# Recurrence products in quarters of the array, stick-breaking value products in halves, in a hybrid decoder layer

## The chip, the cores and the metric

The kernel runs on one core of one Trainium2 chip. The metric is device microseconds (us) of one execution, the median of several. The core has a matrix engine, TensorE (PE in the profile, its weight loads PEld), a vector engine (DVE), a scalar engine (ACT), GpSimd (POOL) and SyncE (SP), which here only issues transfers. Products land in PSUM, which the kernel uses as eight banks of 128 partitions by 512 float32.

## The reference

One decoder layer on x of 1024 tokens by 1024. All three branches read one projection of the normed input.

```python
h = rms_norm(x, norm1_g); proj = h @ w_in            # 1024 x 6912
# A: RWKV-7, 8 heads of 64, state S (64 x 64) per head, per token:
sa = einsum('ij,j->i', S, -kk_t)
S  = S * w_t + sa[:, None] * (kk_t * a_t)[None, :] + v_t[:, None] * k_t[None, :]
y_t = einsum('ij,j->i', S, r_t)                      # then a norm per head, a bonus, a gate
# B: stick-breaking attention, 8 heads of 64, blocks of 128 queries:
attn = where(s < t, exp(log_sigmoid(z) + log_between), 0); o = attn @ v
# M: cross-attention into 256 memory tokens, 4 heads of 128
x = x + (sum_b sigmoid(G_b) * (branch_b @ w_branch[b])) @ w_out
x = x + conv_ffn(rms_norm(x))                        # 1024 -> 2 x 2816 -> 1024
```

## The kernel before

Everything is float32. The large products split each operand into a rounded part and a remainder and add three products (`mm3`); the recurrence, the transposes and the products with attention weights are plain float32 products, each of which the profile shows as two matmul instructions.

The kernel is written as generators. `weave(main, filler, ratio)` runs one step of a main stage and then on average `ratio` steps of a filler: the large projections, gates and branch products, one list of items taken by `pump`. A filler step is in most cases six products of 128x512. `self.pin` keeps TensorE's instructions, and some of DVE's, in the order in which they are written; the other engines' order is left to the scheduler. `need(name)` pumps the filler until an item is done. The stages in order:

- `rwkv_prep`, once for each of four pairs of heads p. A pair sits on 128 partitions, head h2 on partitions 64 h2 to 64 h2 + 63. It builds, for 16 chunks of 64 tokens, decayed keys (`chain`, halves of eight chunks, L373), their Gram products (`gram`, L385, masked by DVE and stored to DRAM as `scr`), and transposes of the values, which ACT's queue stores to `vd` (L365). The strictly lower part goes to `mad`, from which `inverse` computes 128 small triangular inverses on DVE, step by step as the filler advances, and stores them to `td`. Its ratio is 1.
- `sb_attn`, ratio 1.03: a unit is a head (p, h2) and a block b of 128 queries. `front` makes scores and two sigmoids (L791, L792), `weigh` a scan and a product on DVE (L798, L799), `mid` transposes the weights, `back` multiplies them with v, four steps later. `back` uses v of both heads of a pair (128 columns) and keeps one half of the result.
- `mem_attn`, then `stage2`, ratio 2.25: 16 chunks, each with three blocks of products for the four pairs, each block followed by a yield. Block one: the state product `ra[:, 64:128]` with the state U (128 columns, both heads at once; U is kept as 128x128 with zero off-diagonal blocks) plus M times v (L517), copied by DVE (L518). Block two: the inverse `tt` times that (L523), copied by ACT into the lower half of `wv` (L524). Block three: the output (L530, L532) and the state update (L535), with DVE's decayed sum into the new state (L537, once for each head) and ACT's copy of the output (L538). The filler's steps lie between the blocks. Each pair's products in a chunk use one PSUM bank `pb` of the four with the tag `g`. `load` fetches the matrices of two chunks (a group) per pair (L488) and v and the inverses (L491, L492) over SP's queue. `norm_quarter` normalises four chunks at a time among the steps, and `group_norm`, ratio 3, follows.
- `branch_last`, `out_proj`, and the feed-forward phases.

A unit of attention holds two tiles with the tag `at` (seven buffers); the scores and the transposes take `g` banks, one or two each.

## Time and profile before

| | |
|---|---|
| median of 3 runs | 1951.81 us (1951.08 to 1953.57) |
| the profiled execution | 1949.91 us, its span 1948.1 us |
| TensorE busy | 1880.7 us (97%) |
| DVE, ACT, POOL busy | 1246.2, 896.1, 797.2 us |
| mean granted TensorE clock | 0.988 |
| preparation of the recurrence | about 95 to 272 us of the span |
| stick-breaking attention | about 340 to 700 us |
| recurrence | about 832 to 1088 us |

A row of the profile's instructions in order of time gives the start and the length in us, the engine, the line, the operation, what is written from what, the array's rows*columns that a matmul uses, the moving operand's shape and the number of merged instructions. A matmul is in flight longer than its turn lasts, so the distance from one start to the next tells what it costs. Nearly all products go through one helper, so they all have line L112 (transposes L105), and the tiles tell them apart: `g<-it,at` is a product with the state, `g<-qk,at` one with v, `g<-ys,qk` one with the inverse, `g<-qk,qk` a Gram or a score product, and `mm<-at,A` a stick-breaking value product.

### The profile page before, as it was taken

How to read it: one execution, taken by the hardware profiler on the slowest of the kernel's cores; microseconds unless marked ns; L12 is line 12 of the kernel's file. 1: busy time of each engine (PE TensorE's matmuls, PEld its weight loads, DVE VectorE, ACT ScalarE, POOL GpSimd, SP SyncE). 2: the span in 40 equal slices, each digit the busy share in tenths (PEclk: the TensorE clock that was granted, in tenths of full speed). 3: DMA queues.
4: the chain of work that ended last, by engine and by line, in shares of the span. 5: the costliest groups of instructions: out<-in, count | busy, mean ns of one | idle time of the engine just before them, and what ended most of it. 6: DMA issues, size and time to landing. Idle time of an engine off the chain costs nothing. (4 is left out here: it accounts for less than half of the span.)

```text
span 1948.1 us, 27116 instructions
## 1 busy us (share of the span) xinstructions
PE 1880.7 (97%) x10260; PEld 1517.6 (78%) x10260; DVE 1246.2 (64%) x1746; ACT 896.1 (46%) x1585; POOL 797.2 (41%) x458
## 2 busy tenths in 40 slices
PE   8999999999999999899999999989999999999999
PEld 6777777887878887677877877767888888878877
DVE  5666656877878855334443585267677767786496
ACT  5444434665666635423333333354444444455433
POOL 2232333121212434212222353357676767635444
PEclk9999999999999999999999999999999999999999
DMA  4255561111112334576544364223232323277465
GB/s 171 68 170 173 174 205 65 39 49 32 46 50 63 93 100 77 160 253 206 183 132 140 135 212 155 104 87 103 82 113 91 121 81 113 99 279 256 132 227 198
DMA packets 110740, 254.97 MB, mean 131 GB/s; under 512 B 19473, under 2 KB 32017, under 8 KB 110481
## 3 DMA queue, kind: packets, MB, share of 16 engines
q1 hardware_dynamic: 78736, 190.54, 30.3%
q10 hardware_dynamic: 28096, 50.08, 7.2%
q0 software_dynamic: 3776, 12.62, 2.5%
q8 instruction: 81, 1.33, 0.3%
q14 instruction: 51, 0.41, 0.1%
HBM read 175.83 MB, written 77.33 MB: 130 GB/s over the span
## 5 line engine op out<-in xcount | busy, mean ns | idle before, releaser
L81 POOL TENSOR_TENSOR wl<-wr,wh 128x1024 fp32r<-128x1024 f32 x77 | 198.7, 2581 | 527.3 <-ACT wh L80 467.8
L112 PE MATMUL mm<-xhi,wh 128*128 128x512 f32 x784 | 271.8, 427 | 9.8 <-ACT xhi L184 7.8
L112 PE MATMUL mm<-xlo,wh 128*128 128x512 f32 x784 | 249.3, 399 | 0.9 <-DVE xlo L185 0.9
L112 PE MATMUL mm<-xhi,wl 128*128 128x512 f32 x784 | 247.5, 397 | 0.0
L112 PEld LDWEIGHTS mm<-xlo,wh 128*128 128x128 f32 x784 | 149.1, 190 | 37.1 <-DVE xlo L185 1.6
L112 PEld LDWEIGHTS mm<-xhi,wl 128*128 128x128 f32 x784 | 148.6, 190 | 36.2
L112 PEld LDWEIGHTS mm<-xhi,wh 128*128 128x128 f32 x784 | 135.6, 193 | 39.5 <-issue 8.0
L80 ACT ACTIVATE wh<-wr 128x1024 fp32r<-128x1024 f32 x77 | 81.8, 1062 | 160.2 <-PE mm L112 118.6
L112 PE MATMUL mm<-dw,da 128*128 128x512 f32 x528 | 121.6, 390 | 2.4 <-DVE da L1538 2.2
L112 PE MATMUL mm<-BT,l 128*128 128x512 f32 x504 | 119.9, 393 | 0.0
L112 PE MATMUL mm<-BT,wh 128*128 128x512 f32 x352 | 111.5, 398 | 7.7 <-DVE u L1351 7.7
L112 PEld LDWEIGHTS mm<-dw,da 128*128 128x128 f32 x528 | 98.8, 188 | 24.6 <-DVE da L1538 3.5
L1539 POOL TENSOR_TENSOR dw<-draw,dw 128x512 fp32r<-128x512 f32 x55 | 81.1, 1482 | 84.4 <-ACT dw L1537 80.5
L112 PE MATMUL mm<-B,wh 128*128 128x512 f32 x352 | 110.4, 395 | 1.6 <-ACT p L1393 1.6
L112 PEld LDWEIGHTS mm<-BT,l 128*128 128x128 f32 x504 | 94.6, 188 | 22.0
L798 DVE TENSOR_TENSOR_SCAN at<-at,at 128x128 f32<-128x128 f32 (+3 forms) x64 | 94.3, 1474 | 25.3 <-ACT at L792 25.1
L1538 DVE TENSOR_TENSOR da<-draw,da 128x512 fp32r<-128x512 f32 x77 | 64.8, 851 | 60.6 <-ACT da L1536 60.0
L112 PE MATMUL g<-dw,da 128*128 128x512 f32 x396 | 90.8, 390 | 2.3 <-ACT dw L1537 1.2
L1299 POOL TENSOR_TENSOR l<-it,l 128x1024 fp32r<-128x1024 f32 x21 | 50.5, 2407 | 103.5 <-ACT l L1298 103.5
L112 PE MATMUL mm<-at,A 128*128 128x128 f32 (+1 forms) x608 | 91.6, 295 | 1.1 <-DVE qk L964 1.1
L112 PEld LDWEIGHTS mm<-at,A 128*128 128x128 f32 x608 | 80.9, 194 | 10.9 <-issue 3.4
L112 PEld LDWEIGHTS g<-dw,da 128*128 128x128 f32 x396 | 74.2, 188 | 18.4 <-ACT dw L1537 1.6
(322 smaller groups left out, 4226.4 us busy)
## 6 DMA issues: line engine op xcount, KB each, us to landing
wr<-in_w_in_dram SPq DMA_DIRECT2D x50, 512.0 KB, 3.6
draw<-actd SPq DMA_DIRECT2D x77, 256.0 KB, 3.7
at<-scr SPq DMA_DIRECT2D x32, 512.0 KB, 5.6
draw<-in_w_down_dram SPq DMA_DIRECT2D x55, 256.0 KB, 4.7
wr<-in_w_up_dram SPq DMA_DIRECT2D x22, 512.0 KB, 3.5
actd<-gall ACTq DMA_DIRECT2D x44, 256.0 KB, 3.0
rw<-in_w_up_dram SPq DMA_DIRECT2D x20, 512.0 KB, 3.7
actd<-gall ACTq DMA_DIRECT2D x11, 768.0 KB, 3.9
```

Of the source, the lines that this page charges most:

```text
L80: self.nc.scalar.activation(hi, raw, AF.Copy)
L81: self.nc.gpsimd.tensor_tensor(lo, raw, hi.bitcast(F32), ALU.subtract)
L112: self.pinned(self.nc.tensor.matmul(*a, **k))
L798: self.pinned(nc.vector.tensor_tensor_scan(sn[:, :W][:, ::-1], sn[:, :W][:, ::-1], sp[:, :W], 1.0, ALU.mult, ALU.bypass))
L1299: nc.gpsimd.tensor_tensor(lo, src, hi.bitcast(F32), ALU.subtract)
L1538: self.pinned(nc.vector.tensor_tensor(A[:, 1], a, A[:, 0].bitcast(F32), ALU.subtract))
L1539: nc.gpsimd.tensor_tensor(Wt[:, 1], w, Wt[:, 0].bitcast(F32), ALU.subtract)
```

## The change

- Quarters. In `stage2` every product with one head's 64 rows and 64 columns now goes to a quarter of the array: head 0 on rows and columns 0 to 63 and head 1 on 64 to 127 for the state and M products, and crosswise for the inverse. The state products are split by head (64 moving columns instead of 128), the state is kept as 64 columns per pair, and the output products go to column half h2. `heads` lists the heads in plain order, so neighbouring products alternate between quarters. To that end head 1's layout is flipped: `chain` writes b and kp with swapped places for the upper 64 partitions (four DVE products on 64 partitions instead of two on 128), the store to `mad` takes the other half for head 1, and `vd`, `td` and their loads are laid out by head (four stores instead of two for a pair, three loads instead of two). DVE's state update is one instruction for a pair; ACT's copies of `wv` and of the output are two for a pair.
- Halves. `back` runs for two blocks of queries at once, on even units: it uses 64 columns of v and sends block b to column half 0 and block b + 1 to column half 1. The yields of an odd unit stand after `weigh` instead of between `front` and `mid`.
- Order. `gram(0, 1)` goes ahead of `chain(1)`, with one more step ahead of `gram(0, 0)` and one more ahead of `gram(1, 0)`. `stage2` loads v and the inverses of the first group after its first yield, with two more steps ahead of the first chunk.

```diff
-        self.vd = self.pool_d.tile([2, NG, 64, 4, 128], F32, name="vd")
-        self.td = self.pool_d.tile([2, NG, 64, 2, 256], F32, name="td")
+        self.vd = self.pool_d.tile([2, 2, NG, 64, 4, 64], F32, name="vd")
+        self.td = self.pool_d.tile([2, NG, 2, 64, 2, 128], F32, name="td")
...
                 self.transpose(pt[:, j * 128 : (j + 1) * 128], v[:, (h * 4 + j) * 128 : (h * 4 + j + 1) * 128])
             nc.scalar.activation(vt[:, hs], pt, AF.Copy)
         for c2 in range(2):
-            nc.scalar.dma_start(self.vd[p // 2, :, :, p % 2 * 2 + c2].rearrange("g s i -> s g i"), vt[c2 * 64 : c2 * 64 + 64].rearrange("s (g i) -> s g i", g=NG))
+            for h2 in range(2):
+                nc.scalar.dma_start(
+                    self.vd[p // 2, h2, :, :, p % 2 * 2 + c2].rearrange("g s i -> s g i"),
+                    vt[c2 * 64 : c2 * 64 + 64].rearrange("s (g h i) -> s g h i", g=NG, h=2)[:, :, h2])
         for _ in range(2):
             yield
         kk, b = k, a
...
             hs = halves[h]
             bk, ra = self.t4("qk"), self.t4("qk")
             bk4, ra4 = (x.rearrange("p (c u s) -> p c u s", c=8, u=2) for x in (bk, ra))
-            nc.vector.tensor_tensor(bk4[:, :, 0], self.c8(b[:, hs]), self.c8(Q[:, hs]), ALU.mult)
-            nc.vector.tensor_tensor(bk4[:, :, 1], self.c8(kp[:, hs]), self.c8(Q[:, hs]), ALU.mult)
+            for x, first in ((b, 1), (kp, 0)):
+                for h2 in range(2):
+                    q = slice(h2 * 64, h2 * 64 + 64)
+                    nc.vector.tensor_tensor(bk4[q, :, first ^ h2], self.c8(x[q, hs]), self.c8(Q[q, hs]), ALU.mult)
             nc.vector.tensor_tensor(ra4[:, :, 0], self.c8(r[:, hs]), self.c8(P[:, 1 + h * 512 : 1 + (h + 1) * 512]), ALU.mult)
             nc.vector.scalar_tensor_tensor(ra4[:, :, 1], self.c8(P[:, hs]), -1.0, self.c8(kk[:, hs]), ALU.mult, ALU.mult)
             nc.vector.tensor_scalar(ra4[:, :, 1, 0], self.c8(kk[:, hs])[:, :, 0], -math.exp(OFF), None, ALU.mult)
...
                 self.scr[p, g0 : g0 + 2, :, 512:1024].rearrange("g q c -> q g c"), mt.rearrange("q (g c) -> q g c", g=2))
             for h2 in range(2):
                 i0 = p * 32 + h2 * 16 + h * 8 + f * 4
-                nc.sync.dma_start(self.mad[i0 : i0 + 4].rearrange("c s t -> s c t"), mt4[0:64, :, h2, 64:128])
+                nc.sync.dma_start(self.mad[i0 : i0 + 4].rearrange("c s t -> s c t"), mt4[64 - h2 * 64 : 128 - h2 * 64, :, h2, 64:128])
 
         def decayed(h, bk):
             bp = self.t4("it")
...
         nc.sync.dma_start(self.ggd[p, 1], bon)
         nc.scalar.activation(g, g, AF.Copy, scale=self.par("lnx_g", p))
         nc.scalar.dma_start(self.ggd[p, 0], g)
-        for _ in range(3):
+        for _ in range(4):
             yield
         gram(0, 0, *u0)
-        u1 = chain(1)
         yield
         gram(0, 1, *u0)
+        u1 = chain(1)
         for _ in range(2):
             yield
         turned(0, bp)
         bp = decayed(1, u1[0])
-        for _ in range(3):
+        for _ in range(4):
             yield
         gram(1, 0, *u1)
         yield
...
             for h2 in range(2):
                 for cc in range(2):
                     i0 = p * 32 + h2 * 16 + cc
-                    nc.gpsimd.dma_start(self.td[p // 2, :, :, p % 2, cc * 128 + h2 * 64 : cc * 128 + h2 * 64 + 64], X[i0 : i0 + 15 : 2])
+                    nc.gpsimd.dma_start(self.td[p // 2, :, h2, :, p % 2, cc * 64 : cc * 64 + 64], X[i0 : i0 + 15 : 2])
 
     def stage2(self):
         nc = self.nc
         self.y = [self.t4("qk") for _ in range(4)]
         vs = self.t4("ys", n=512)
-        ut = self.t4("it").rearrange("p (u c) -> p u c", u=8)
+        ut = self.t4("it")[:, 0:512].rearrange("p (u c) -> p u c", u=8)
         U = [[ut[:, 2 * p + i] for i in range(2)] for p in range(4)]
-        for p in range(4):
-            for i in range(2):
-                nc.gpsimd.memset(U[p][i], 0.0)
+        nc.gpsimd.memset(ut, 0.0)
         hq = [slice(0, 64), slice(64, 128)]
+        heads = [(p, h2) for p in range(4) for h2 in range(2)]
+        A, Y, W, S = (slice(o, o + 64) for o in range(0, 256, 64))
         Ls, VTs = {}, {}
         norm = iter(())
 
...
                 nc.sync.dma_start(Ls[g, p], self.scr[p, g])
             if "V" in what and p % 2 == 0:
                 V2 = self.t4("qk")
-                nc.sync.dma_start(V2[64:128, 0:512], self.vd[p // 2, g].rearrange("s c i -> s (c i)"))
-                nc.sync.dma_start(V2[0:64, 512:1024], self.td[p // 2, g].rearrange("s p i -> s (p i)"))
+                for h2 in range(2):
+                    nc.sync.dma_start(V2[hq[h2], h2 * 256 : h2 * 256 + 256], self.vd[p // 2, h2, g].rearrange("s c i -> s (c i)"))
+                nc.sync.dma_start(V2[:, 512:768], self.td[p // 2, g].rearrange("h s p i -> (h s) (p i)"))
                 for i in range(2):
-                    VTs[g, p + i] = V2.rearrange("s (u p i) -> s u p i", u=2, p=2)[:, :, i]
-
-        for what in "LV":
-            for p in range(4):
-                load(0, p, what)
+                    VTs[g, p + i] = [V2[:, h2 * 256 + i * 128 : h2 * 256 + i * 128 + 128] for h2 in range(2)], V2[:, 512 + i * 128 : 640 + i * 128]
+
+        for p in range(4):
+            load(0, p, "L")
         yield
+        for p in range(0, 4, 2):
+            load(0, p, "V")
+        for _ in range(2):
+            yield
         for c in range(NC):
             g, cc = c // 2, c % 2
             if cc and g + 1 < NG:
...
                     load(g + 1, p)
             us = []
             for p in range(4):
-                L, VT = Ls[g, p], VTs[g, p]
+                L, (V, TT) = Ls[g, p], VTs[g, p]
                 us.append((
                     U[p][cc], U[p][1 - cc], L[:, cc * 128 : (cc + 1) * 128], L[:, 256 + cc * 128 : 256 + (cc + 1) * 128],
-                    L[:, 512 + cc * 256 : 512 + (cc + 1) * 256], VT[:, 0, cc * 128 : (cc + 1) * 128],
-                    VT[0:64, 1, cc * 128 : (cc + 1) * 128], vs[0:64, p * 128 : (p + 1) * 128], self.ps("g")))
-            if c:
-                for Uo, Un, ra, bt, M, wv, tt, v1, pb in us:
-                    self.mmul(pb[0:64, 0:128], ra[:, 64:128], Uo, start=True, stop=False)
-            for Uo, Un, ra, bt, M, wv, tt, v1, pb in us:
+                    L[:, 512 + cc * 256 : 512 + (cc + 1) * 256], [v[:, cc * 64 : (cc + 1) * 64] for v in V],
+                    TT[:, cc * 64 : (cc + 1) * 64], vs[:, p * 64 : (p + 1) * 64], self.ps("g")))
+
+            def state(o, rs):
+                for p, h2 in heads if c else ():
+                    Uo, _, ra, _, _, _, _, _, pb = us[p]
+                    q = hq[h2]
+                    self.mmul(pb[q, o], ra[q, rs], Uo[q], start=True, stop=False)
+
+            state(A, Y)
+            for p, h2 in heads:
+                _, _, _, _, M, wv, _, v1, pb = us[p]
+                self.mmul(pb[hq[h2], A], M[hq[h2], h2 * 128 + 64 : h2 * 128 + 128], wv[h2][hq[h2]], start=(c == 0), stop=True)
+                if h2 == 1:
+                    nc.vector.tensor_copy(v1, pb[:, A])
+            yield
+            next(norm, None)
+            for p, h2 in heads:
+                _, _, _, _, _, wv, tt, v1, pb = us[p]
+                self.mmul(pb[hq[1 - h2], W], tt[hq[h2]], v1[hq[h2]], start=True, stop=True)
+                if h2 == 1:
+                    for q, w in zip(hq, wv[::-1]):
+                        nc.scalar.activation(w[q], pb[q, W], AF.Copy)
+            yield
+            next(norm, None)
+            state(Y, A)
+            for p, (Uo, Un, ra, bt, M, wv, tt, v1, pb) in enumerate(us):
                 for h2, q in enumerate(hq):
-                    self.mmul(pb[0:64, q], M[64:128, h2 * 128 + 64 : h2 * 128 + 128], wv[64:128, q], start=(c == 0), stop=(c == 0 or h2 == 1))
-                nc.vector.tensor_copy(v1, pb[0:64, 0:128])
-            yield
-            next(norm, None)
-            for Uo, Un, ra, bt, M, wv, tt, v1, pb in us:
-                for h2, q in enumerate(hq):
-                    self.mmul(pb[0:64, 128 + h2 * 64 : 192 + h2 * 64], tt[:, q], v1[:, q], start=True, stop=True)
-                nc.scalar.activation(wv[0:64], pb[0:64, 128:256], AF.Copy)
-            yield
-            next(norm, None)
-            for p, (Uo, Un, ra, bt, M, wv, tt, v1, pb) in enumerate(us):
-                yo = pb[cc * 64 : cc * 64 + 64, 320:448]
-                if c:
-                    self.mmul(yo, ra[:, 0:64], Uo, start=True, stop=False)
-                for h2, q in enumerate(hq):
-                    self.mmul(yo[:, q], M[:, h2 * 128 : h2 * 128 + 64], wv[:, q], start=(c == 0), stop=(c == 0 or h2 == 1))
+                    self.mmul(pb[q, Y], M[:, h2 * 128 : h2 * 128 + 64], wv[h2], start=(c == 0), stop=True)
                 if c < NC - 1:
                     for h2, q in enumerate(hq):
-                        self.mmul(pb[q, 256:320], bt[:, q], wv[:, q], start=True, stop=True)
-                    for h2, q in enumerate(hq):
-                        nc.vector.scalar_tensor_tensor(Un[q, q], Uo[q, q], self.pc[p][q, c : c + 1], pb[q, 256:320], ALU.mult, ALU.add)
-                nc.scalar.activation(self.y[p][cc * 64 : cc * 64 + 64, g * 128 : (g + 1) * 128], yo, AF.Copy)
+                        self.mmul(pb[q, S], bt[:, q], wv[h2], start=True, stop=True)
+                    nc.vector.scalar_tensor_tensor(Un, Uo, self.pc[p][:, c : c + 1], pb[:, S], ALU.mult, ALU.add)
+                for h2, q in enumerate(hq):
+                    nc.scalar.activation(self.y[p][cc * 64 : cc * 64 + 64, g * 128 + h2 * 64 : g * 128 + h2 * 64 + 64], pb[q, Y], AF.Copy)
             if cc and g + 1 < NG:
                 load(g + 1, 3)
             yield
...
 
         def back(u):
             p, half, h2, b = units[u]
-            q = slice(h2 * 64, h2 * 64 + 64)
-            at, _ = st.pop(u)
+            ats = [st.pop(u + i)[0] for i in range(2)]
             if b % 4 == 0:
                 st["py"] = self.ps("mm")
             py = st["py"]
-            for j in range(b + 1):
-                vo = (j % 2) * 512 + p * 128
-                self.mmul(
-                    py[:, (b % 4) * 128 : (b % 4 + 1) * 128], self.v[j // 2][:, vo : vo + 128], at[:, j * 128 : (j + 1) * 128],
-                    start=(j == 0), stop=(j == b))
-            if b % 4 == 3:
-                hs = slice(half * 512, (half + 1) * 512)
+            ts = slice(b % 4 * 64, b % 4 * 64 + 128)
+            for j in range(b + 2):
+                vo = (j % 2) * 512 + p * 128 + h2 * 64
+                for i, at in enumerate(ats):
+                    if j <= b + i:
+                        self.mmul(
+                            py[i * 64 : i * 64 + 64, ts], self.v[j // 2][:, vo : vo + 64], at[:, j * 128 : (j + 1) * 128],
+                            start=(j == 0), stop=(j == b + i))
+            if b % 4 == 2:
+                q = slice(h2 * 64, h2 * 64 + 64)
                 y = self.t4("ys", n=512)
-                nc.scalar.activation(y[q], py[q], AF.Copy)
-                nc.scalar.dma_start(self.yd[1, p, q, hs], y[q])
+                for i in range(2):
+                    nc.scalar.activation(
+                        y[q].rearrange("c (b i t) -> c b i t", b=2, i=2)[:, :, i],
+                        py[i * 64 : i * 64 + 64, 0:256].rearrange("c (b t) -> c b t", b=2), AF.Copy)
+                nc.scalar.dma_start(self.yd[1, p, q, half * 512 : (half + 1) * 512], y[q])
 
         for u in range(len(units) + 4):
-            if u >= 4:
-                back(u - 4)
-            if u < len(units):
+            if u % 2 == 0:
+                if u >= 4:
+                    back(u - 4)
+                if u < len(units):
+                    front(u)
+                yield
+            elif u < len(units):
                 front(u)
-            yield
             if 2 <= u < len(units) + 2:
                 mid(u - 2)
             if u < len(units):
                 weigh(u)
             yield
+            if u % 2:
+                yield
 
     def mem_kv(self):
         nc = self.nc
```

## Prediction

> **What bounds the kernel now.** I read the page first, then the stretches of the span by stage, then TensorE's waits, then TensorE's instructions in order of time in the stages that the change touches.
>
> ```profile
> span 1948.1 us, 27116 instructions
> PE 1880.7 (97%) x10260; PEld 1517.6 (78%) x10260; DVE 1246.2 (64%) x1746; ACT 896.1 (46%) x1585; POOL 797.2 (41%) x458
> ```
>
> TensorE (PE) is busy for 97% of the span and the next engine for 64%. A busy PE is not a PE at its peak, so the question is whether its busy time can be made denser, and whether what feeds it keeps up.
>
> ```profile
> 95.00:272.00 177.00, 173.07 (x1018) 131.12 (x1016) 110.29 (x138) 75.03 (x92) 61.99 (x27) 1.00 0.59 186
> 360.00:700.00 340.00, 328.42 (x2154) 280.10 (x2153) 268.56 (x242) 212.26 (x380) 87.90 (x38) 0.97 0.20 61
> 832.00:1085.00 253.00, 245.23 (x1843) 196.08 (x1841) 107.25 (x288) 82.85 (x259) 58.79 (x34) 0.97 0.52 173
> ...
> PE g L105 <- DVE at L799: 10.7, 4, 3.9
> PE g L112 <- ACT qk L538: 5.4, 9, 1.7
> PE g L112 <- DMA at<-scr: 2.4, 1, 2.4
> ```
>
> These stretches are the preparation of the recurrence, stick-breaking attention and the recurrence (columns: length, then busy time of PE, PE's weight loads, DVE, ACT, POOL, then clock). PE fills all three: what leaves its stream shortens the span, unless a wait takes its place. DVE, at 268.56 of 340 us in attention, is the one engine near it; PE already waits 10.7 us for DVE's L799 there, and 7.8 us in the recurrence.
>
> **Recurrence, now.** One of the 16 chunks, with the woven products (mm) around its three blocks:
>
> ```profile
> 1002.16 0.63 PE L112 MATMUL mm<-xhi,wl 128*128 128x512 f32 x2
> ...
> 1003.33 0.38 PE L112 MATMUL g<-it,at 128*64 128x128 f32 x2
> 1003.55 0.51 PE L112 MATMUL g<-qk,at 128*64 128x64 f32 x8
> 1003.90 0.38 PE L112 MATMUL g<-it,at 128*64 128x128 f32 x2
> ...
> 1005.13 0.73 PE L112 MATMUL mm<-xhi,wh 128*128 128x512 f32 x2
> 1005.69 0.63 PE L112 MATMUL mm<-xlo,wh 128*128 128x512 f32 x2
> 1006.16 0.63 PE L112 MATMUL mm<-xhi,wl 128*128 128x512 f32 x2
> ...
> 1007.54 0.63 PE L112 MATMUL mm<-yhi,wl 128*128 128x512 f32 x2
> 1008.10 1.09 PE L112 MATMUL g<-it,at 128*64 128x128 f32 x8
> 1009.12 1.14 PE L112 MATMUL g<-qk,at 64*64 64x64 f32 x16
> 1010.19 0.73 PE L112 MATMUL mm<-yhi,wh 128*128 128x512 f32 x2
> 1010.75 0.62 PE L112 MATMUL mm<-A,wh 128*128 128x512 f32 x2
> ...
> 1012.58 0.63 PE L112 MATMUL mm<-yhi,wl 128*128 128x512 f32 x2
> 1013.14 1.14 PE L112 MATMUL g<-ys,qk 64*64 64x64 f32 x16
> 1014.21 0.72 PE L112 MATMUL mm<-yhi,wh 128*128 128x512 f32 x2
> 1014.77 0.63 PE L112 MATMUL mm<-A,wh 128*128 128x512 f32 x2
> ```
>
> Each float32 product is two instructions. Undisturbed, a woven pair takes 0.47 us (1005.69 to 1006.16). So the block that starts at 1008.10 (state products, then L517) costs from 1007.54 + 0.47 to 1010.75 - 0.47: 2.27 us. The next (L523) costs 1.25 us, and the first (output and state update) 2.59 us: 6.1 us in all.
>
> What is in them: an instruction with 128 moving columns takes 0.11 us (1003.33 to 1003.55, two). The eight 64-column ones take 0.35 us (1003.55 to 1003.90); the first four all write one half of the columns of the array, the last four alternate between its halves. If one alone takes 0.058 us and alternating ones share that slot two by two, the eight take 4 x 0.058 + 2 x 0.058 = 0.35, as measured; unshared they would take 0.46. In 1009.12 to 1010.19 sixteen that all sit in one quarter of the array take 1.07 us: 16 x 0.058 = 0.93, and the end of the block. So the blocks hold 1.81, 0.93 and 2.28 us of slots. The rest (0.46, 0.32, 0.31) is going into and out of a split array: about 0.32 a block, and 0.13 more where the first block changes from halves to quarters.
>
> Does sharing hold for 128 columns and for halves of the rows? The Gram products alternate between row halves:
>
> ```profile
> 94.07 1.16 PE L112 MATMUL g<-qk,qk 64*128 64x128 f32 x16
> 95.16 0.73 PE L112 MATMUL mm<-xhi,wh 128*128 128x512 f32 x2
> ```
>
> Sixteen instructions with 128 columns take 1.09 us, where 16 x 0.11 = 1.76 would be due one by one: they share too, but their halves write two banks of PSUM. No row shows quarters on the diagonal in one bank, which the change makes of it.
>
> **Recurrence, after.** State products: 4 of 128 columns become 8 in diagonal quarters of 64, before both L517 and the output. With sharing, the blocks are: 32 instructions in 16 slots, 0.93 + 0.32 = 1.25 us; 8 slots, 0.46 + 0.32 = 0.78; 8 slots of state, 0.13 for the change of split, 16 slots of output and update, 0.32: 1.84. Sum 3.87 against 6.1: 2.2 us a chunk, 33 us over 15 chunks, and 1.4 for the first, which has no state products (three times 8 slots): **34.8 us** (15 x 2.23 + 1.4).
>
> The Trainium skill, page "TensorEngine Tiling (Array Packing)", section "Restrictions and Gotchas", speaks against this: different row tiles cannot use one PSUM bank at the same time. Diagonal quarters are different row tiles in one bank; the S products above share a bank but not rows, so no row decides. By that rule the quarters would take turns, the first rival below.
>
> **Stick-breaking values.**
>
> ```profile
> 505.35 1.06 PE L112 MATMUL mm<-at,A 128*128 128x128 f32 x8
> 506.16 0.48 PE L112 MATMUL g<-qk,qk 128*128 128x256 f32 x2
> ...
> 516.61 1.95 PE L112 MATMUL mm<-at,A 128*128 128x128 f32 x16
> 518.31 0.70 PE L112 MATMUL g<-qk,qk 128*128 128x512 f32 x2
> ```
>
> A block of n instructions takes 0.111 n - 0.08 us (0.81 for 8, 1.70 for 16). Per head the eight blocks hold 2, 4, ... 16, 72 in all: 7.35 us, 8 heads 58.8 us. After, two blocks share the column halves: each step j is one shared product of two instructions, b + 2 steps for the pair (b, b+1): 4, 8, 12, 16 slots of 0.11 = 4.4 us a head, and four entries and exits of 0.32, which the full array did not pay: 5.7 us, 8 heads 45.4. **13.4 us** saved (24 if the entries were free).
>
> The Trainium skill, page "TensorE: Matmul & The Clock Gate", section "Packing small matmuls — row/col tiling", has weight loads overlap running products only in different row groups; column halves have the same one, so by it the pairs would not share, the third rival. The 0.35 us above speaks against it, for 64 columns.
>
> **What is given back.** Attention: PE stands shorter between a scan and the transpose that needs it. DVE goes from 79% to 82% of 327 us. A wait there costs twice:
>
> ```profile
> 463.38 1.94 PE L105 MATMUL g<-kon,at 128*128 128x128 f32 x8 [3.87 <-DVE at L799]
> ...
> 465.97 1.05 PE L112 MATMUL mm<-xlo,wh 128*128 128x512 f32 x2
> 466.82 1.05 PE L112 MATMUL mm<-xhi,wl 128*128 128x512 f32 x2
> ```
>
> After 3.87 us of waiting a pair takes 0.85 us instead of 0.47: the clock was halved. Between the first unit of a head and the last one's transpose, three double blocks save about half a microsecond; over 8 heads that is 4 us more waiting if DVE is the end of each, 0 to 15 us with the clock. In odd units `front` and `mid` now follow each other with nothing woven between, so `g` banks come round sooner: 3 us (0 to 8).
>
> ```profile
> L378 DVE TENSOR_TENSOR qk<-qk,qk x8: 679/682/2876, 79.8 to 252.1; 128x512 f32<-128x512 f32 x8
> L537 DVE SCALAR_TENSOR_TENSOR it<-it,pc,g x120: 260/281/290, 840.8 to 1075.3; 64x64 f32<-64x64 f32 x120
> L538 ACT ACTIVATE qk<-g x64: 253/272/275, 841.5 to 1088.2; 64x128 f32<-64x128 f32 x64
> at<-scr SPq DMA_DIRECT2D x32, 512.0 KB, 5.6
> ...
> 1127.04 1.03 PE L105 MATMUL g<-kon,qk 128*128 128x128 f32 x8
> 1136.22 2.02 PE L112 MATMUL mm<-at,wh 128*128 128x512 f32 x8
> ```
>
> (L378 is a product of a chain, L537 the state update and L538 the output's copy, each with minimum, median and maximum in ns; then the load of a group's matrices, with the us to landing; then the last transposes of the norm and the first products of the last branch.)
>
> Recurrence: DVE's updates halve (60 x 0.28 = 17 us less, on the path only behind the norms). ACT's copies L524 and L538 double: 128 more of half the size, at most 0.27 us each, 35 us on 83 of 253. They lie under the 2.25 woven steps after each block (a step is 3 pairs of 0.47, so 3.2 us): the eight copies of a block take at most 2.2 us. If that cover is gone, PE waits for the operand of its next block, or for the bank. The fourth load of a group goes out when the first pair's output is done (1003.33) and is needed in the next state block (1008.10 and three of its four pairs, 1008.87); these 5.5 us shrink by 1.3, and a load lands in 5.6 in the median. Yet PE waited for it once. The first v loads are now queued on SP behind the weight and gate loads, two steps (4.5 woven steps, 6.3 us) ahead of the first chunk, and 16 more v loads pass SP. All this: 3 us (-3, since the shorter DVE chain shortens L538's waits, to 10).
>
> End: those two steps use up 4.5 woven steps that now fill the 9.2 us from the last transposes (1127.04) to the last branch (1136.22). 6.3 of them go, and the DVE and ACT work under them shows in part: 2 us (0 to 6).
>
> Preparation: two more DVE products in each of 8 chains, half the partitions at the same length: 16 x 0.68 = 10.9 us on 110 of 177. The second chain, with its DVE products and its SP store, goes behind one more set of Gram products, masks and three SP stores, and has the same six steps ahead of its own Gram products. Eight more small v stores go through ACT's queue. PE's 4 idle us here say that this is covered; without cover it is 11 us. The two more steps per pair take woven work that the run up to the first attention unit would do anyway. I count 0 (0 to 4).
>
> Sum: 34.8 + 13.4 - 4 - 3 - 3 - 2 = 36 us. The profiled execution took 1949.91 us (its span 1948.1 and 1.8 around it), 1.9 below the median of 1951.81; I take the 36 from the median: **1916 us**.
>
> **Rivals.** One: diagonal quarters in one bank take turns. Blocks then cost 32, 16 and 16 slots of 0.058 and the 16 shared ones: 2.18, 1.25 and 2.31 us, 5.74 against 6.1. The recurrence gives 6 us instead of 34.8 and the total is 1952 - 6 - 13.4 + 12 = 1944. For it: the Gram products' separate banks; against: the quarters write different partitions. Two, slower: ACT becomes the recurrence's bound. Its in-order queue also holds the woven work's evacuations, so each doubled set of copies comes late. If the 35 us of added copies lie wholly on PE's path and every second chunk's wait halves the clock for 6.8 us (8 x 3.4 = 27 us), the total is 1916 + 35 + 27 = 1978. It decides from about 0.75 us of wait at each of 48 hand-overs (36 us). Against: ACT would be at 118 of some 218 us. Three: column halves do not share with 128 columns. Values then cost 576 x 0.11 + 10.2 = 74 us, 15 more than now, and the total is 1952 - 34.8 + 15 + 12 = 1944. Four: waits of DVE, ACT and clock eat the gain evenly and nothing shows, 1950.
>
> **How the numbers follow.** Forecast 0.72, rival one 0.12, three 0.04, slower 0.08, no change 0.04. The forecast's own range is 1896 (free entries for the values, 10 us, and 10 of the 15 us between the costs and their low ends) to 1940 (costs of 36 of the 43 us that their high ends make). I let the range reach 1946 to take in rivals one and three; left out are the slower case, no change and the tails, about 2 in 10. A measurement here can tell 0.2%, 4 us, from no change. Faster: nearly all of the forecast, most of one and three, 0.84; same 0.05; slower, with the tails of the others, 0.11.
>
> **What would show it.** Right: per chunk, blocks of about 1.25, 0.8 and 1.85 us, with quarter instructions at 0.03 us; value blocks of 16 slots near 2.1 us for the last two units instead of 3.2; PE's busy time some 45 us lower, its waits some 10 us higher. Wrong: blocks near 2.2 and 1.25 us (rival one); long waits on the two L524 or L538 copies (two); value blocks over 3.5 us (three); or a drop of the granted clock in attention that follows new waits on L799.

## The result and the profile after

The changed kernel took 1929.62 us, median of 4 runs (1926.05 to 1935.56), against 1951.44 for the kernel before beside it: a ratio of 0.989 (95% interval 0.9861 to 0.9919), 21.8 us faster. The forecast was 1916, 36 us faster, with a range of 1896 to 1946. So the direction and the range held, and 14 us of the forecast gain are missing. The profiled execution took 1926.05 us, the fastest of the four.

The page of the changed kernel, and its stretches (length, busy time of PE, PE's weight loads, DVE, ACT and POOL, granted clock, DMA share, GB/s):

```profile
span 1924.3 us, 27682 instructions
PE 1834.8 (95%) x10500; PEld 1455.7 (76%) x10500; DVE 1230.2 (64%) x1702; ACT 922.4 (48%) x1729; POOL 791.7 (41%) x451
```

```profile
360.00:700.00 340.00, 317.35 (x2184) 253.21 (x2183) 277.50 (x243) 215.97 (x400) 89.04 (x38) 0.98 0.20 61
...
809.60:848.80 39.20, 25.08 (x92) 17.80 (x90) 9.17 (x11) 10.64 (x12) 9.74 (x9) 0.74 0.79 232
```

PE's busy time fell by 45.9 us, as forecast, and the span by only 23.8: PE stands 22.1 us longer, where some 10 were expected. The last stretch shows where most of that happens. It is the transition, from the last cross-attention product to the first product with an inverse, and in it PE is busy for 25 of 39 us at a clock of 0.74. In the kernel before, the same stretch looks like this:

```profile
822.80:835.70 12.90, 12.90 (x66) 9.92 (x64) 6.91 (x8) 5.47 (x7) 2.40 (x1) 1.00 0.81 306
```

Cut at the same products in both profiles, the stages (us) are:

| stage | before | after | change |
|---|---|---|---|
| preparation, to the first score product | 330.1 | 334.2 | +4.1 |
| attention and cross-attention | 492.7 | 475.4 | -17.3 |
| transition | 12.9 | 39.2 | +26.3 |
| recurrence, to the last state product | 252.0 | 220.9 | -31.1 |
| norms, to the last branch's first product | 48.5 | 41.9 | -6.6 |
| last branch | 147.6 | 152.3 | +4.7 |
| feed-forward | 664.3 | 660.3 | -4.0 |

The feed-forward code is unchanged, and its up phase came out at 440 to 447 us in the profiles of the kernels below. So the 4.0 us in the last row are not the change's.

**The recurrence did what was forecast.** One of its chunks in the changed kernel, in order of time:

```profile
991.21 0.63 PE L112 MATMUL mm<-yhi,wl 128*128 128x512 f32 x2
991.76 0.68 PE L112 MATMUL g<-ys,qk 64*64 64x64 f32 x16
992.38 0.73 PE L112 MATMUL mm<-yhi,wh 128*128 128x512 f32 x2
992.94 0.62 PE L112 MATMUL mm<-A,wh 128*128 128x512 f32 x2
...
994.77 0.63 PE L112 MATMUL mm<-yhi,wl 128*128 128x512 f32 x2
995.33 0.68 PE L112 MATMUL g<-it,at 64*64 64x64 f32 x16
995.94 1.15 PE L112 MATMUL g<-qk,at 128*64 128x64 f32 x32
997.02 0.74 PE L112 MATMUL mm<-yhi,wh 128*128 128x512 f32 x2
997.60 0.62 PE L112 MATMUL mm<-A,wh 128*128 128x512 f32 x2
...
999.44 0.63 PE L112 MATMUL mm<-xhi,wl 128*128 128x512 f32 x2
999.99 0.68 PE L112 MATMUL g<-it,at 64*64 64x64 f32 x16
1000.51 0.63 PE L112 MATMUL g<-qk,at 64*64 64x64 f32 x16
1001.07 0.74 PE L112 MATMUL mm<-xhi,wh 128*128 128x512 f32 x2
1001.65 0.63 PE L112 MATMUL mm<-xlo,wh 128*128 128x512 f32 x2
```

The sixteen inverse products take 0.62 us (991.76 to 992.38); in one quarter they took 1.07. The 32 instructions of state and M products take 1.08. Counted as the prediction counted them, from the end of the woven pair before to where an undisturbed one would follow, the blocks cost 0.79 us (forecast 0.78), 1.89 (1.84) and 1.27 (1.25). Diagonal quarters in one bank share their slots fully here; the Trainium skill's rule against it ("TensorEngine Tiling (Array Packing)", "Restrictions and Gotchas") did not hold for these quarters, which write different partitions.

**The value blocks too.** One of the double blocks of the last two units of a head:

```profile
596.59 0.62 PE L112 MATMUL mm<-xhi,wl 128*128 128x512 f32 x2
597.14 1.97 PE L112 MATMUL mm<-at,A 128*64 128x128 f32 x30
599.04 0.61 PE L112 MATMUL g<-qk,qk 128*128 128x384 f32 x2
```

Thirty instructions take 1.98 us (596.59 and 0.47 to 599.04) where 2.1 was forecast and 3.3 would be due one by one at 0.11. DVE stands at 277.50 of 340 us in attention, 82%, as forecast.

### The profile page after: what moved, and what is told of

Its sections match the earlier page's. It is cut to its first block, busy times and chain, and to the rows that moved or that the text cites. A ratio compares the mean times of both kernels' runs of the same rounds, so it can differ in the third digit from the quotient of the medians.

```text
span 1924.3 us, 27682 instructions
## 1 busy us (share of the span) xinstructions
PE 1834.8 (95%) x10500; PEld 1455.7 (76%) x10500; DVE 1230.2 (64%) x1702; ACT 922.4 (48%) x1729; POOL 791.7 (41%) x451
## 5 line engine op out<-in xcount | busy, mean ns | idle before, releaser
L81 POOL TENSOR_TENSOR wl<-wr,wh 128x1024 fp32r<-128x1024 f32 x77 | 200.7, 2607 | 542.4 <-ACT wh L80 526.7
L112 PEld LDWEIGHTS mm<-dw,da 128*128 128x128 f32 x528 | 98.9, 188 | 23.3 <-DVE da L1563 2.3
L1561 ACT ACTIVATE da<-draw 128x512 fp32r<-128x512 f32 x77 | 48.3, 629 | 84.3 <-PE mm L112 40.9
L112 PEld LDWEIGHTS mm<-BT,wh 128*128 128x128 f32 x352 | 65.9, 188 | 19.7 <-DVE u L1376 4.3
```

What stands on the lines that cost most here:

```text
L81: self.nc.gpsimd.tensor_tensor(lo, raw, hi.bitcast(F32), ALU.subtract)
L112: self.pinned(self.nc.tensor.matmul(*a, **k))
L1561: self.pinned(nc.scalar.activation(A[:, 0], a, AF.Copy))
```

## Where the missing gain went: reading the transition

TensorE's waits of the changed kernel (total, times, longest). L814 is DVE's product in `weigh` (L799 before), L825 ACT's copy of the transposed weights (L810 before), L400 DVE's mask of the Gram products (L395 before), L1111 the gating product of a branch, and L1040, below, ACT's copy of the transposed probabilities in cross-attention (L1015 before):

```profile
PE mm L112 <- ACT yhi L1073: 12.7, 2, 9.5
PE g L105 <- DVE at L814: 12.1, 6, 4.1
...
PE mm L112 <- DVE w L1111: 5.0, 1, 5.0
PE g L105 <- DVE at L400: 4.9, 3, 2.0
```

The first is new. `yhi` is the rounded part of the branch's input (`split_y`), and its tile has the tag `inst`: it uses the one buffer in which `inverse` works. It can be written only when the last store of the inverses has read that buffer. Here are the inverse's sums (minimum, median, maximum in ns, first and last start) and its stores, in the kernel before:

```profile
L463 DVE TENSOR_TENSOR inst<-inst,it x62: 226/967/3142, 280.5 to 757.0; 128x62 f32<-128x62 f32 x2, 128x122 f32<-128x122 f32 x2, 128x180 f32<-128x180 f32 x2, 128x236 f32<-128x236 f32 x2
...
L470 POOL DMA_DIRECT2D td<-inst x16: 787/818/923, 757.6 to 777.5; - x16
```

and in the changed kernel:

```profile
L468 DVE TENSOR_TENSOR inst<-inst,it x62: 224/994/3216, 296.0 to 794.5; 128x62 f32<-128x62 f32 x2, 128x122 f32<-128x122 f32 x2, 128x180 f32<-128x180 f32 x2, 128x236 f32<-128x236 f32 x2
...
L475 POOL DMA_DIRECT2D td<-inst x16: 798/798/913, 795.1 to 814.8; - x16
```

What follows on ACT, and then on PE, in order of time:

```profile
826.95 1.99 ACT L1073 ACTIVATE yhi<-w 128x1024 fp32r<-128x1024 f32 x2
...
839.47 1.06 ACT L1073 ACTIVATE yhi<-w 128x1024 fp32r<-128x1024 f32 x1 [5.04 <-DMA w<-yd]
```

```profile
828.05 1.22 PE L112 MATMUL mm<-yhi,wh 128*128 128x512 f32 x2 [9.47 <-ACT yhi L1073]
...
840.58 1.22 PE L112 MATMUL mm<-yhi,wh 128*128 128x512 f32 x2 [3.25 <-ACT yhi L1073]
```

The inverse ends 37.5 us later, so do its stores. The last one starts at 814.8 and lands 10.9 us later, at 825.7, and the first split starts at 826.95. The second wait, 3.25 us, is another: there the split stands on the load of its input (`w<-yd`), which SyncE issued at 831.5.

The cause is in the steps: `inverse` advances by 0.8 of a step for each filler step between the end of the preparation and `sb0`. The two steps added per pair use up eight filler steps before that stretch. From the inverse's first instruction to the first score product TensorE has 148 `mm` instructions, where it had 197: some eight filler steps of six fewer. By that product 21 of the inverse's 124 instructions have started, where it had been 28, and the inverse makes them up at half a step for each filler step.

## The experiments

All times are medians; ratios are to the kernel before, run beside each on the same chip (1951.3 to 1952.4 us), with 95% intervals.

**The inverse's start put back.**

```diff
-        pace[0] = 8
+        pace[0] = 10
```

> The changed kernel with one number changed: the inverse advances by 10 tenths of a step per woven step between the preparation and the first attention unit, not 8. The two more steps per pair in the preparation took 8 woven steps out of that stretch, so the inverse got some 26 of its 124 steps there instead of 33; with 10 tenths it gets 33 again. Theory (the inverse is late, and what hangs on it holds up PE at the start of the recurrence): the inverse's last update at 794 us of the span and its stores at 795 to 815 come 15 to 35 us earlier, the 12.7 us that PE waits for the splits of the branch inputs and the half clock after it go, and the time is 1905 to 1914. Rival (the first v loads and the two added steps on SP's queue hold it up): the inverse is earlier, the wait stays, and the time is 1926 to 1932.

Measured: 1924.91 us, 0.9863 (0.9845 to 0.9881). The inverse's last sum starts at 756.4, the transition falls to 18.0 us with PE busy throughout, and the time still lies above the 1905 to 1914 of the theory:

```profile
824.20:842.20 18.00, 18.00 (x92) 13.93 (x90) 9.10 (x11) 6.55 (x9) 3.05 (x2) 1.00 0.79 281
```

But attention and cross-attention grow by 13.9, to 489.3 us, and the gain on the changed kernel is 4.7, which is not clear of noise: the two intervals overlap. Two waits pay for it: 15.9 us instead of 12.1 on L814, and one that the changed kernel had lost with its late inverse and that the kernel before had too (there L1015):

```profile
PE g L112 <- ACT at L1040: 6.4, 1, 6.4
```

**Is it ACT's queue instead?** A rival for the late split: ACT stands on a `ys` buffer, of which there is one (its copy L1050 waits 9.14 us just ahead of the split). In `mem_attn`:

```diff
-            y = self.t4("ys", n=512)
+            y = self.t4("at")[:, :512]
```

> The changed kernel, but the outputs of the cross-attention are copied into a buffer of the seven with the tag at instead of the single one with the tag ys; the inverse stays as late as it is. Theory A (ACT's queue is what holds PE: its copy of an attention output waits 9 us for the only ys buffer, whose store lands late among the inverse's stores, and the splits of the branch inputs stand behind it): ACT's 16.3 us of waiting for these stores go, PE's 12.7 us shrink to under 4, and the time is 1910 to 1920. Theory B (the split inputs need the buffer that the inverse's matrices occupy until their stores have landed, at about 826 us): the first split still starts at about 826 us, and the time is within 3 us of the changed kernel, 1926 to 1932.

Measured: 1933.6 us, 0.9906 (0.9891 to 0.9921); the wait on L1073 stays, 18.1 us with 12.6 the longest. The rival falls. ACT's queue is now free ahead of the split, and the split shows what it waits for: the last store of the inverses starts at 817.9 and lands 12.5 us later, at 830.4. The load that the row names had landed at 825.5, so it did not end the wait.

```profile
830.59 2.95 ACT L1073 ACTIVATE yhi<-w 128x1024 fp32r<-128x1024 f32 x3 [10.79 <-DMA at<-scr]
```

**Halves alone**: the kernel before with the changed `back` and its loop, nothing else.

> The kernel before with the stick-breaking value products in halves alone (the changed back and its loop), without the quarters and the new order. By the prediction's steps (13.4 us less, 7 us of new waits): 6 us faster, 1945. By the trace of the changed kernel, where the stretch from the first score product to the last value product is 13.8 us shorter: 1937 to 1940.

Measured: 1944.58 us, 0.9971 (0.9957 to 0.9985): 6.7 us, the figure of the prediction's steps and not that of the trace. DVE's L799 is now waited for 12.8 us in 6 waits, 10.7 in 4 before. The profile is of the fastest of the twelve executions (1937.85), so it does not show all that the median gave back.

**The change without halves**: the changed kernel with the old `back` and loop.

> The changed kernel with the value products of before on the full array: quarters and new order alone. If the parts add up, the halves' share comes off: 1935 to 1943 (6 to 14 us slower than the changed kernel). If the inverse's lateness is the common cause, the longer attention lets the inverse end earlier against the recurrence, its wait shrinks, and the time is below 1935.

Measured: 1931.97 us, 0.9901 (0.9882 to 0.992). Here the halves bring 2.4 us of the forecast 6.4, which the noise does not tell from nothing; in the profiles attention and cross-attention are 2.3 us shorter with them (475.4 against 477.7). The time is below 1935, but not for the reason given: the inverse's last sum starts at 799.0, and the split, which starts at 831.7 after 2.18 us on the stores `td<-inst`, is waited for 14.0 us, no less than with halves. With them PE waits 12.1 us on L814 and 4.7 on ACT's L825, without them:

```profile
PE g L105 <- DVE at L814: 4.2, 3, 2.5
...
PE g L105 <- ACT at L825: 2.1, 1, 2.1
```

**Both repairs**: pace 10 and the other buffer.

> The earlier inverse (10 tenths) and the other buffer for the cross-attention's outputs together. With the earlier inverse alone the wait at the recurrence's start was gone (the stretch from the last cross-attention product to the first inverse product fell from 39.2 to 18.0 us), but the inverse's stores met the cross-attention's again and PE waited 6.4 us there. Theory (that meeting costs what the earlier inverse wins, through the single ys buffer): the 6.4 us go, cross-attention's stretch falls from 135.5 to about 126 us, and the time is 1913 to 1919. Rival (the buffer is not the point, the stores themselves hold up the transfers): PE still waits over 4 us there and the time is 1922 to 1927.

Measured: 1925.94 us, 0.9864 (0.9848 to 0.988). The L1040 wait of 6.4 us is still there, so the buffer is not its cause either, as the rival had it. The time is that of pace 10 alone.

**v loaded early again**, on top of that:

```diff
-        yield
         for p in range(0, 4, 2):
             load(0, p, "V")
-        for _ in range(2):
-            yield
+        yield
```

> The kernel of the run before this one, and the first v loads back ahead of the recurrence's first step, without the two added steps. Theory (the two steps take cover from the end): PE's 5.0 us of waiting for DVE in the last branch, and the half clock after it, go; the stretch before the first inverse product is some 6 us shorter and the one from the last output product to the last branch some 6 us longer; the time is 5 to 9 us below the run before it. Rival (the two steps are neutral, the wait at the end has another cause): within 3 us of it, with the 5.0 us still there.

Measured: 1937.39 us, 0.9919 (0.9905 to 0.9934): 11 us slower, the theory was wrong. The last branch came back from 152.3 to 147.7 us as expected, but the recurrence now waits for the copies of the output and for the group loads:

```profile
PE g L112 <- DMA at<-scr: 9.6, 7, 4.1
PE g L112 <- ACT qk L551: 9.2, 4, 3.8
```

The recurrence stage took 224.3 us in the run before it, here 229.4, and the transition did not shrink (18.0, here 19.5) though the woven work of two steps left it for the norms' stage (41.9, here 48.8). So the later loads and the two steps pay for themselves; the two were not tried apart.

**The old order of the preparation**: the changed kernel with `chain(1)` between its Gram products and three steps for four.

> The changed kernel with the preparation's order of before: the second chain between the two Gram products, three steps instead of four at the two places, the inverse's pace at 8 tenths; the four products of a chain stay. Woven steps and inverse steps ahead of attention are then as before the change. If the order costs the 4.1 us by which attention starts later: it starts at 330 us. If the two more DVE products of each chain do: it starts at 334 or later, with 5 us or more of PE waiting for DVE's L400 and chains. In both cases the inverse is back at its old place, and what follows is as with the earlier inverse: 1920 to 1928.

Measured: 1931.51 us, 0.9894 (0.9872 to 0.9916). The transition is 18.0 us as with pace 10, but attention starts at 340.2, later than with the new order (334.2). So the new order does not cost the 4.1 us of the preparation; more likely it hides part of the added DVE products: PE waits 4.4 us on L400 here, and 4.8 on the chain's L386 where it had been 1.5. The added products were not tried alone. This late start is part of why the time misses the 1920 to 1928 expected. The run also shows the cause at work from the other side: with the eight steps back and the pace left at 8, the inverse's last sum starts at 760.7.

**Without the inverse.** Three kernels leave out nearly all of its DVE work:

```diff
-        for s in range(1, 63):
+        for s in range(1, 2):
```

> The changed kernel with 122 of the inverse's 124 DVE instructions left out (its output is not the reference's). Theory A, the missing part of the forecast is the inverse's doing (it ends 37 us later, holds the buffer of the branch split, and its DVE steps stand beside attention): without it the changed kernel keeps its gains whole, so it lies 36 to 46 us under the kernel before with the same left out (next run). Stage from the last cross-attention product to the first inverse product near 18 us instead of 39, attention and cross-attention shorter than after's 475 by the waits on the softmax differences. Rival B, the gains were lost elsewhere (preparation, end, recurrence): the difference of the two stays near 22 us.

> The kernel before with the same 122 DVE instructions left out (its output is not the reference's). Both theories: it loses its DVE waits in attention (8.2 us on L799 and the half clock behind them, 24 us in attention and cross-attention, some 12 us of span) and comes to 1930 to 1945. Theory A: e8 lies 36 to 46 us below this run; rival B: near 22 us below.

> The changed kernel with the value products of before and with the same 122 DVE instructions left out (its output is not the reference's). Theory A: with DVE unloaded the halves' shorter blocks are no longer given back in waits, so e8 lies 9 to 13 us below this run. Rival B: the halves' two-unit step (two scores ahead, one g bank less) causes the waits by itself, inverse or not, and e8 lies 0 to 4 us below.

| | with inverse | without | |
|---|---|---|---|
| before | 1951.4 | 1942.20 (1940.4 to 1947.76) | 0.9959 (0.9946 to 0.9972) |
| changed, no halves | 1932.0 | 1920.43 (1916.62 to 1923.67) | 0.9842 (0.9828 to 0.9857) |
| changed | 1929.6 | 1907.25 (1904.3 to 1910.12) | 0.9778 (0.9765 to 0.9791) |
| gain of the whole change | 21.8 | 35.0 | |
| gain of the halves in it | 2.4 | 13.2 | |

Without the inverse the change is worth 35.0 us, beside a forecast of 36 and 1 short of the range expected of this run; the halves alone 13.2, beside a term of 13.4. The rivals expected 22 and 0 to 4. So what is missing goes with the inverse. The agreement to 1 us does not hold term by term. Against the kernel before without the inverse, attention and cross-attention are 12.9 us shorter (474.6 to 461.7) where the terms make 6.4. From the transition to the last branch the stages are together 23.3 us shorter where the terms make 29.8. The two misses of 6.5 us cancel. Attention and cross-attention, first of the changed kernel, then of it without the inverse:

```profile
334.20:809.60 475.40, 450.75 (x2972) 358.23 (x2972) 354.05 (x391) 287.33 (x551) 131.77 (x70) 0.99 0.22 68
```

```profile
342.30:804.00 461.70, 446.68 (x2971) 355.07 (x2971) 248.41 (x285) 291.07 (x556) 119.92 (x56) 1.00 0.22 70
```

DVE has 106 us less to do there, PE stands for 15.0 us instead of 24.7, and the transition takes 18.0 us again. Even so the halves give something back: without them, and without the inverse, PE stands for 8.0 us in this stage and waits for ACT's L825 not at all, with them 8.9 us. So their price is in part their own, as the second rival has it, and of their 13.2 us this stage gives 10.4 and the preparation, which they do not touch, 2.1.

These kernels also start attention some 8 to 12 us later, the one before as well, and this hides the 4.1 us of the preparation (342.1 and 342.3). There the sixteen stores come at once, from 281.6 in the kernel before without the inverse, and the weight splits L81 stand behind them on GpSimd:

```profile
302.83 1.22 PE L112 MATMUL mm<-xhi,wl 128*128 128x512 f32 x2 [8.67 <-POOL wl L81]
```

**Half of the inverse on GpSimd**, to unload DVE without leaving anything out:

```diff
-            self.pinned(nc.vector.tensor_tensor(tv, ...))
+            self.pinned(nc.gpsimd.tensor_tensor(tv, ...))
```

> The changed kernel with the inverse's 62 product instructions on GpSimd and its 62 sums left on DVE. Theory A: DVE loses some 60 us of work beside attention, the waits on the softmax differences (12.1 us) shrink, and the time falls by 5 to 15 us under the changed kernel if GpSimd takes under 3 us for a product. Rival B: GpSimd's products (1024 elements took 2.6 us there, L81) hold up the weight splits queued behind them and the inverse ends later still: no gain or a loss of up to 15 us.

Measured: 1948.12 us, 0.9979 (0.9965 to 0.9992), 18.5 slower than the changed kernel, beyond the 15 of the rival. The products take 1.69 us in the median where DVE took 0.95, and the cost is not the one the rival named (L81 is waited for 2.5 us). DVE stands for the product, and attention's scan and product stand behind that on DVE's queue. What DVE's sums waited for (us, times), and what PE waited for:

```profile
  POOL it L466: 53.1, 20
```

```profile
PE g L105 <- DVE at L814: 21.4, 6, 7.0
PE mm L112 <- ACT yhi L1073: 16.8, 2, 11.6
```

**The stores on SyncE**, with pace 10, after the L1040 wait was read in the run with pace 10 and the other buffer. There the stores stand in GpSimd's queue from 757.45, and it ends:

```profile
776.60 2.39 POOL L81 TENSOR_TENSOR wl<-wr,wh 128x1024 fp32r<-128x1024 f32 x1
778.92 0.82 POOL L475 DMA_DIRECT2D td<-inst  x1
779.77 1.67 POOL L171 TENSOR_TENSOR hf<-rs,half 128x8 f32<-128x8 f32 x1
789.13 2.35 POOL L81 TENSOR_TENSOR wl<-wr,wh 128x1024 fp32r<-128x1024 f32 x1 [7.70 <-ACT wh L80]
791.43 1.19 POOL L661 TENSOR_TENSOR hf<-hf,rsc 128x8 f32<-128x8 f32 x1
```

The query norm of the next cross-attention head (L171, L661) is done at 792.6, behind the stores and a split; the softmax needs it, and PE's product at 796.58 has waited 6.44 us for L1040. Most of the delay is the split between L171 and L661, which waits 7.70 us for ACT.

```diff
-                    nc.gpsimd.dma_start(self.td[...], X[i0 : i0 + 15 : 2])
+                    nc.sync.dma_start(self.td[...], X[i0 : i0 + 15 : 2])
```

> The changed kernel with the inverse's pace put back from 8 to 10 tenths in the stretch before attention (as in the run e1_pace10) and its sixteen stores issued by SyncE instead of GpSimd. Theory: the wait of 6.4 us on the probabilities' copies L1040 in cross-attention, and the half clock behind it (6.8 us, some 3.4 us of span), come from those stores, which keep GpSimd's queue from 758.9 to 780.3 in e1 while the query norm's power (L171, L661) and the weight split stand behind them. On SyncE the wait goes: 8 to 11 us under e1's 1924.9, that is 1913 to 1918, and the stretch from the last cross-attention product to the first inverse product stays at 18 us. Rival: the wait is the gate's activation table between two softmax pieces on ScalarE, which stays wherever the stores are issued; the time stays at 1921 to 1929. Second rival: SyncE then stands on the inverse with weight loads behind it, waits on the weight split L81 grow, and the time is 1925 to 1940.

Measured: 1943.0 us, 0.9949 (0.9934 to 0.9965). The L1040 wait is gone and attention with cross-attention is 8.2 us shorter than with pace 10 alone (481.1 against 489.3), as the theory said, and the table load as a cause falls. GpSimd's queue now reads:

```profile
778.82 1.68 POOL L171 TENSOR_TENSOR hf<-rs,half 128x8 f32<-128x8 f32 x1 [8.06 <-DVE rs L170]
780.58 0.20 POOL L661 TENSOR_TENSOR hf<-hf,rsc 128x8 f32<-128x8 f32 x1
```

L171 starts only 1 us earlier than in the rows above, since it now waits for DVE. What went is the split between the two. As these rows read, the stores cost this wait less by the time that they take than by the order that GpSimd's queue has with them; another order alone was not tried.

But the second rival is right too, above its price: the sixteen stores stretch over 70 us of SyncE's queue, and the weight load behind them comes late to the transition, which takes 41.7 us. (This profile is of the slowest of nine executions, 1950.21.) SyncE's queue, its waits ahead of the stores, and PE:

```profile
756.30 69.55 SPq L475 DMA_DIRECT2D td<-inst  x16
...
829.17 0.38 SPq L76 DMA_DIRECT2D wr<-in_w_br_dram  x1
```

```profile
SPq L475 <- DMA gsd<-w: 28.9, 2, 23.3
SPq L475 <- DMA yd<-ys: 26.3, 4, 14.1
```

```profile
837.30 1.22 PE L112 MATMUL mm<-yhi,wh 128*128 128x512 f32 x2 [12.85 <-ACT wh L80]
```

A store itself takes SyncE 0.65 us in the median. Some 55 of the 70 us are waits that the profile puts down to ACT's stores of the gates and of the attention outputs; why the stores stand on those is not shown.

Of the kernels that compute everything, pace 10 alone (1924.9) is the fastest, with the other buffer beside it 1 us behind, within noise.

## Why the prediction was right, and what it missed

- **Recurrence, 34.8 less 3: right.** The blocks came out within 0.05 us each and the stage gave 31.1. ACT's doubled copies stayed hidden (4.3 us of waits on the output's copy L553 where L538 had 5.4); rivals one and two fall.
- **Values, 13.4: right in size, lost in place.** Column halves share with 128 columns: a block of thirty took 1.98 us where 2.1 was forecast. Rival three falls, and with it the prediction's reading of the rule on weight loads. That the halves are worth 13.2 us without the inverse is partly luck: the stage gives 10.4 of it.
- **Attention's price, 4 + 3: right for the halves alone, too small in the whole.** The halves alone kept 6.7, as the forecast 13.4 - 7 has it. In the whole change they kept 2.4: the waits on L814 and L825 took 10.5 us more than without them. Part of the price is not DVE's: ACT's L825, which the terms do not name, is waited for even without the inverse.
- **The step that was wrong** is in the preparation: "The two more steps per pair take woven work that the run up to the first attention unit would do anyway. I count 0". That work is done anyway, but its steps are also the clock of `inverse`. Eight fewer of them in the paced stretch put its end 37.5 us back, onto the buffer of the branch split. The transition grew by 26.3 us. 5.1 of them are the woven work of the two added steps at the start of `stage2` (18.0 us with pace 10, PE busy throughout, against 12.9), which the norms' stage gave back (-6.6). The other 21.2 are 14.1 us of standing and products slowed by half clock.
- **Why this did not cost 21, and where luck came in.** The late inverse also took its stores out of cross-attention, and with them the 6.4 us wait on L1040 and the half clock behind it. This explains most of why attention and cross-attention gained 17.3 us where the terms make 6.4, and why putting the inverse back (pace 10) brings 4.7 us and not 21: it costs 13.9 there. The prediction had neither effect, and that they half cancel is luck. Without the 10.9 us gained beyond the terms the time would lie, by estimate, near 1940, the end of the range that the forecast's own costs gave.
- **Preparation, 0 (0 to 4)**: 4.1, at the edge of its bounds, with L400 waited for 4.9 us where L395 had 2.5. **End, 2 (0 to 6)**: the last branch is 4.7 us longer, 5.0 of waiting for L1111 and half clock behind it. It is inside its bounds, and returned when the v loads went early again.

In short: the blocks on TensorE came out as forecast, and 13 us of the gain went with the inverse, whose pace the added steps changed. That the sum without the inverse meets the forecast to 1 us is luck, since two misses of 6.5 us cancel in it. From the transition on 6.5 us are missing: mostly the recurrence, 28.4 us shorter where 31.8 was forecast, and the last branch, 6.6 longer where 2 was, with 7.2 of waiting for L1111. Why these differ stays open. The inverse's 106 us on DVE beside attention and its stores would always have stood somewhere; whether a placement exists that costs much less than the 17.7 us between pace 10 and no inverse at all stays open. GpSimd for the products and SyncE for the stores were both worse.

## What to carry to other kernels

When steps of a woven schedule are added or moved, list everything that advances by those steps, not only the work that the steps carry: a background task paced by them ends later, and its buffers and stores come free later. Removing work from TensorE where another engine is near it gives back only what that engine can follow; running the kernel with the other engine's background work left out sizes this, if the result is read stage by stage and not by the total alone. Stores in a row stand in the queue that issues them, with all that they wait for, so look at what comes behind them before they are moved.

## What was not expected of the hardware

The sixteen stores of the inverses (each eight matrices, in rows of 64 numbers) stretch over 20 us of their queue on GpSimd (757.6 to 777.5 in the kernel before, at some 0.8 us a store and 6.5 us of waits for their own transfers). On SyncE they stretch over 70 us, of which some 55 are waits. And short waits of PE are followed by half clock: in the transition of the changed kernel 14 us of standing came with a mean clock of 0.74 over 39 us, where the same stretch without the wait (pace 10) took 18.0 us at 1.00. By the granted clock of the changed kernel's trace nine waits of 1.95 to 9.5 us were each followed by 3.4 to 13.7 us at half clock, while two others of 1.98 and 2.83 us were not.
